# A hybrid two-layer encoder step on one core: the SSM layer's first cluster, its exponents and its state scaling are re-ordered

## The chip, the cores and the metric

The kernel runs on one core of a Trainium2 chip. The metric is the time of one execution on the device, in microseconds (us). A kernel's time is the median of its runs.

A core has a matrix engine (TensorE, PE in the profile), a vector engine (VectorE, DVE), a scalar engine (ScalarE, ACT), a general engine (GpSimd, POOL), and queues that start transfers. Each engine works through its own list of instructions in order. An instruction that waits for another engine holds up everything behind it in its list.

## The reference

The model is one inference step of two layers for 384 tokens: 256 tokens of one prompt and 8 sample streams of 16 tokens. Layer 0 is a gated short convolution beside attention. Layer 1, which the change touches, is a state-space (SSM) mixer in four groups of eight heads. Each layer ends in a convolutional feed-forward. Of layer 1's mixer:

```python
z, xbc, dt_raw = split(h @ w_in)
xbc = silu(causal_dwconv(xbc))              # x: 16 tiles of 128 features, B: 4, C: 4
dt = softplus(dt_raw + dt_bias)
cum = cumsum(dt * a)                        # per head
mix = (C B^T) * exp(cum_q - cum_k) * dt     # causal, inside a chunk
y   = mix @ x + exp(cum) * (C h_in)         # h_in: state that enters the chunk
h   = exp(cum_end) * h + (B * w_end)^T x    # state that leaves it
y   = (y + d_skip * x) * silu(z)
out = rms_norm(y, per group) @ w_out
```

The prompt is worked as two blocks of 128 tokens (b = 0, 1), the eight samples together as a third block (b = 2). Each sample has a state of its own, 128 x 512 values in a group, which is read, scaled, added to and written back.

## The kernel before

All large products are in three parts (high and low halves of activations and weights), so each weight tile of 1,024 columns is split into `wh` (ACT) and `wl` (DVE, line 300) as it arrives. A feature-major product (`xbc`, 24 matmuls of 384 columns) uses one such tile. A `z` projection (72 matmuls of 512 columns) uses four.

Instructions of TensorE in the SSM layer stay in the order of the program text (`T.keep`). Those of the other engines are put in order when the kernel is built, by priority, which is their place in the text unless `tc.high_priority()` raises it.

PSUM has eight banks: three for the large products (`pmm`) and five for all the rest (`paux`), each used in turn. A product therefore waits until the bank's earlier content has been read out ("evicted").

The layer begins with the convolutions of B and C of group 0 (`conv_bc`) and of the first three x tiles (`conv_x`). Then come the exponents: `E` (from `dA` and a masked copy `dAm`), `cT`, whose result goes to memory in `rows` and is read back spread over the partitions as the four `td` tiles (`decays`), and `sgS` from `tjd`. Then `turn_bc(0)`: the products `cb`, evicted into `CB` by DVE, and the transposes `bT`. Then the fourth x tile, B and C of group 1, and `turn_x`, which transposes the four x tiles (`xT`).

Then a loop runs over the groups. In a group, in this order on TensorE:

- the transposes `yT` of the gated output of the group before (`Gate.turn`: read out by ACT into `yh` and by DVE into `yl`);
- `within`: the prompt's state products `S` and the products `y` of each block;
- `inter(2)`: the samples' part `yi`, which reads the eight sample states `h0`;
- `inter(1)`, `turn_bc` and convolutions of the next group, with half of the output product `op` of the group before in group 1;
- `states(0)` and `states(1)`: products `hn`, four banks each. POOL scales a state by its exponent, DVE adds `hn`, and ACT starts the store `o_hs`;
- `project_z` (`z`), then `turn_x`, the scale of the gated output (`factor`), the rest of `op`, and B and C of the group after next.

`skip` loads the next eight states into the same eight buffers and lets POOL make `y` from `xt` and the skip weights. A convolution's `pad` (DVE, from PSUM), its three multiply-adds `c` (DVE, line 303) and its `silu` (ACT, `xf`) follow each `xbc`.

Of the kernel before, what the change touches and what calls it, by code (L numbers as in the profile page):

```python
# [10 lines left out]
F32 = mybir.dt.float32  # L11
# [71 lines left out]
def _pack(x):  # L83
# [47 lines left out]
                blocks.append(wo[kt * P:(kt + 1) * P, c:c + 256])  # L131

    bc(0, 0), bc(1, 0), xs(0), bc(0, 1), bc(1, 1), xs(1), tm(wi, 0)
    bc(0, 2), bc(1, 2), xs(2, (0,)), out(0, (0, 256)), xs(2, (1, 2, 3)), tm(wi, 512), out(0, (512, 768))
    bc(0, 3), bc(1, 3), xs(3), tm(wi, 1024), out(1), tm(wi, 1536), out(2), out(3)
    ffn(1)
    w = np.concatenate(blocks, 1)
# [93 lines left out]
def build(nc, tc, d, stop=None):  # L231
# [119 lines left out]
    class Weights:  # L351
        def __init__(self):
            self.tiles, self.made, self.raw, self.pos = {}, 0, None, 0

            t, self.gain = 32 + 3 * NF + 8, {}
            for g, at in enumerate(((11, 12, 20, 21), range(32, 36), range(40, 44), range(44, 48))):
                self.gain.update({t + i: 4 * g for i in at})
            self.total = d["w"].shape[0] * (RC // WC)

# [620 lines left out]
    def turn_bc(g, Bg, Cg):  # L980

        ps = paux("cb")
        for b in range(3):
            o = slice(b * P, (b + 1) * P)
            T.matmul(ps[:, o], lhsT=Bg[:, o], rhs=Cg[:, o], start=True, stop=True)
        CB = t512("CB", 2, (P, 3, P))
        tt(CB[:, 0:2, :], ps[:, 0:256].rearrange("p (b q) -> p b q", q=P),
           C("T").unsqueeze(1).broadcast_to([P, 2, P]), ALU.mult)
        tt(CB[:, 2, :], ps[:, 256:384], C("Ts"), ALU.mult)
        ps = paux("bT")  # L990
        for b in range(3):
            T.transpose(ps[:, b * P:(b + 1) * P], Bg[:, b * P:(b + 1) * P], ident)
        Bt = t512("Bt", 2, (P, 2, P))
        act(Bt, ps[:, :256].rearrange("p (b n) -> p b n", n=P), AF.Copy)

        Bm = t512("Bm", 2, (P, 2, P))
        for par in range(2):
            act(Bm[:, par, :], ps[:, 256:384], AF.Copy, scale=C("pmask")[:, par:par + 1])
        Cm = Cms[g % 2]
        c4 = Cg[:, 256:384].rearrange("p (j two t) -> p j two t", two=2, t=LB)  # L1000
        for two in range(2):
            G.tensor_copy(Cm[:, two::2, 16 * two:16 * two + 16], c4[:, :, two, :])
        return Cg, Cm, CB, Bt, Bm
# [30 lines left out]
    class Group:  # L1034
# [31 lines left out]
        def skip(self):  # L1066

            self.h0 = []
            for bb in range(NB):
                h0 = t512("h0", 8)  # L1070
                nc.sync.dma_start(out=h0, in_=d["h0"][bb, self.g])
                self.h0.append(h0)
            for b in range(3):
                y = t512("y", 5)
                tt(heads(y[:, :]), heads(self.xt[:, b, :]), bc64(prr("dsk", 32)[:, self.h8]), ALU.mult, G)
                self.ys.append(y)

        def within(self):

            g = self.g  # L1080
            for b in range(3):
                if b < 2:
                    ph = paux("S")
                    T.matmul(ph, lhsT=self.Bt[:, b, :], rhs=self.xw[b], start=True, stop=True)
                    if b == 0:
                        self.S0 = t512("S0", 1)
                        act(self.S0, ph, AF.Copy)
                    else:
                        S1 = self.xt[:, 0, :]
                        tt(heads(S1), heads(self.S0[:, :]), bc64(E[:, 224 + 8 * g:232 + 8 * g]), ALU.mult)  # L1090
                        tt(S1, S1, ph, ALU.add)
                        nc.gpsimd.dma_start(out=d["o_hp"][g], in_=S1)
                py = paux("y")
                for h in range(8):
                    for half in range(2):
                        q = slice(64 * half, 64 * half + 64)
                        T.matmul(py[q, 64 * h:64 * h + 64], lhsT=self.mix[b][h // 4][:, h % 4, q],
                                 rhs=self.xdt[b][:, 64 * h:64 * h + 64], start=True, stop=True)
                tt(self.ys[b], self.ys[b], py, ALU.add)

        def inter(self, b, late=False):

            pi = paux("yi")
            if b == 1:
                T.matmul(pi, lhsT=self.Cg[:, P:2 * P], rhs=self.S0, start=True, stop=True)
            else:

                for par in range(2):
                    for i in range(4):
                        T.matmul(pi[32 * i:32 * i + 32, :], lhsT=self.Cm[:, 2 * i + par, :], rhs=self.h0[2 * i + par],  # L1110
                                 start=par == 0, stop=par == 1)
            yi = self.xt[:, b, :]
            tt(heads(yi), heads(pi[:, :]), bc64(self.col(E, b)), ALU.mult)
            tt(self.ys[b], self.ys[b], yi, ALU.add, None if late else G)

        def states(self, par):

            ph = [paux("hn") for _ in range(4)]
            for i in range(4):
                rows = slice(32 * i, 32 * i + 32)  # L1120
                T.matmul(ph[i], lhsT=self.Bm[rows, par, :], rhs=self.xw[2][rows, :], start=True, stop=True)
            for i in range(4):
                bb = 2 * i + par
                h0, o = self.h0[bb], 256 + 32 * bb + 8 * self.g
                tt(heads(h0[:, :]), heads(h0[:, :]), bc64(E[:, o:o + 8]), ALU.mult, G)
                tt(h0, h0, ph[i], ALU.add)
                nc.scalar.dma_start(out=d["o_hs"][bb, self.g], in_=h0)

# [16 lines left out]
    class Gate:  # L1145
# [13 lines left out]
        def part(self, b, zs):  # L1159
            y = self.ys[b]  # L1160
            tt(y, y, zs[:, b, :], ALU.mult)
            act(t512("yi", 1), y, AF.Square, accum_out=self.ssq[:, b:b + 1])

        def factor(self):
            v = tiny.tile([P, 3], F32, tag="v", name="v")
# [10 lines left out]
        def turn(self, b):  # L1176
            ps = to_features(self.ys[b], "yT")
            o = slice(b * P, (b + 1) * P)
            if self.late:
                for i in range(4):  # L1180
                    yh, yl = self.y2[0][i][:, o], self.y2[1][i][:, o]
                    act(yh, ps[:, i, :], AF.Copy)
                    tt(yl, ps[:, i, :], f32(yh), ALU.subtract)
            else:
                yh, yl = self.y3
                act(yh[:, :, o], ps, AF.Copy)
                tt(yl[:, :, o], ps, f32(yh[:, :, o]), ALU.subtract)

    def add_out(yh, yl, factor):
        for m0 in range(0, 8, 2):  # L1190
            ws = [W.take(256) for _ in range(4)]
            for m in range(2):
# [6 lines left out]
                if factor is None:  # L1199
                    residual(m0 + m, ps)  # L1200
                else:
                    o = t512("y", 5, (P, NT))
                    tt(o, ps[:, :NT], factor, ALU.mult)
                    tt(X[:, m0 + m, :], X[:, m0 + m, :], o, ALU.add)
                    norm_tile(m0 + m, "g_ffn", 1, o1)
# [12 lines left out]
    T.keep = True  # L1218
    Cn = conv_bc(1, 0)
    xs = [conv_x(0, i) for i in range(3)]  # L1220
    dAm = t512("h0", 8, (P, NB, 32))
    tt(dAm, dA[:, 64:96].unsqueeze(1).broadcast_to([P, NB, 32]),
       C("bmask").unsqueeze(2).broadcast_to([P, NB, 32]), ALU.mult)
# [8 lines left out]

    cumK = o0.tile([P, 64], F32, name="cumK")
    V.tensor_copy(cumK, ps[:, 0:64])
    ps = paux("cT")
    for b in range(2):
        T.matmul(ps[0:32, b * P:(b + 1) * P], lhsT=dA[:, 32 * b:32 * b + 32], rhs=C("T"), start=True, stop=True)
    cumQ = o1.tile([32, 256], F32, tag="pad", name="cumQ")
    V.tensor_copy(cumQ, ps[0:32, 0:256])
    rows = dram.tile([2, 32, P], F32, name="rows")  # L1240
    nc.sync.dma_start(out=rows.rearrange("b h q -> h b q"), in_=cumQ.rearrange("h (b q) -> h b q", q=P))
    tt(wdt, E[:, 96:192], dt, ALU.mult)
    tjd = t512("h0", 8, (P, 32, LB))
    tt(tjd, dA[:, 64:96].unsqueeze(2).broadcast_to([P, 32, LB]),
# [3 lines left out]
    act(decS, ps, AF.Exp)  # L1248

    decs = decays(0)  # L1250
    grp = Group(0, decs, turn_bc(0, Bn, Cn))
    xs.append(conv_x(0, 3))
    Bn, Cn = conv_bc(0, 1), conv_bc(1, 1)
    grp.take(turn_x(xs))
    grp.skip()
    xs = [conv_x(1, 0)]
    op = gate = None
    for g in range(4):
        if gate:
            for b in range(3):  # L1260
                gate.turn(b)
            op = add_out(*gate.y2, None)
        last = g == 3
        grp.within()
        grp.inter(2, last)
        if last:
            break
        decs = decays(g + 1)
        if g == 0:
            xs.append(conv_x(1, 1))  # L1270
        elif g == 1:
            steps(op, 16)
        else:
            xs = [conv_x(g + 1, 0)]
        grp.inter(1)
        bc_ = turn_bc(g + 1, Bn, Cn)
        xs.append(conv_x(g + 1, len(xs)))
        grp.states(0)
        while len(xs) < 4:
            xs.append(conv_x(g + 1, len(xs)))  # L1280
        grp.states(1)
        nxt = Group(g + 1, decs, bc_)
        zs = run(project_z())
        gate = Gate(grp.ys, False)
        for b in range(3):
            gate.part(b, zs)
# [5 lines left out]
            steps(op)  # L1292
        if g < 2:
            Bn, Cn = conv_bc(0, g + 2), conv_bc(1, g + 2)
        if g == 0:
            xs = [conv_x(2, 0)]
        grp.skip()

    z = project_z()
# [40 lines left out]
```

## Time and profile before

| what | us |
|---|---|
| runs | 1081.5, 1085.78, 1085.08 |
| median | 1085.08 |
| the profiled execution | 1087.0 |
| its span, first to last instruction | 1085.1 |

The span is the stretch that the profile's rows cover. The profiled execution's own time is 1.9 us longer. Row times count from the span's start. A row's last bracket is the time its engine was idle just before it, and what ended that. "PEclk" is the TensorE clock that was granted, as a share of 2.4 GHz.

### The profile page before, as it was taken

The page shows a single profiled execution, that of the slowest core. Times are in us where ns is not written, and L with a number is a line of the kernel's source. Part 1 is how long each engine was busy: PE and PEld are TensorE (multiplying, and loading weights), DVE is VectorE, ACT ScalarE, POOL GpSimd, SP SyncE. Part 2 cuts the span into 40 slices and gives each one's busy share as a digit, 9 for nine tenths or more (in the row PEclk, how much of TensorE's full clock was granted, in tenths as well). Part 3 has the DMA queues.
Part 4 walks back from the last instruction along what each step waited for, and adds up shares of the span by engine and source line. Part 5 has one row for each costly group of instructions (what it writes and reads, how often), then busy time and mean ns, then how long its engine had stood idle before and what let it go on. Part 6 is the DMA issues. An engine that isn't in the chain of part 4 may idle for free.

```text
span 1085.1 us, 16777 instructions
## 1 busy us (share of the span) xinstructions
PE 1048.3 (97%) x6316; PEld 974.8 (90%) x6316; DVE 739.6 (68%) x1329; ACT 493.6 (45%) x817; POOL 161.7 (15%) x383
## 2 busy tenths in 40 slices
PE   9999999999999999997898999999999999999998
PEld 6788899999999999986776877797899999999998
DVE  7968557776777543486888877975897676765332
ACT  6344334544444433347636556462554444443221
POOL 0030000100000000031824524424001000000000
PEclk9999999999999999998999999999999999999999
DMA  8542443443434444436274363453534434434441
GB/s 281 155 149 72 158 136 117 128 133 120 132 122 132 133 127 128 126 108 187 77 237 150 123 219 127 159 185 106 175 119 123 135 117 125 129 118 143 139 150 42
DMA packets 50328, 150.30 MB, mean 139 GB/s; under 512 B 5992, under 2 KB 8312, under 8 KB 50248
## 3 DMA queue, kind: packets, MB, share of 16 engines
q1 hardware_dynamic: 44360, 136.78, 40.5%
q10 hardware_dynamic: 4608, 8.39, 2.0%
q0 software_dynamic: 1280, 4.06, 1.0%
q8 instruction: 50, 0.82, 0.3%
q14 instruction: 30, 0.25, 0.1%
HBM read 135.81 MB, written 13.40 MB: 138 GB/s over the span
## 4 chain that ended last, share of the span: by engine, by line
PE 37%; DVE 13%; ACT 3%; issue 2%; DMA 2%; SPq 0%; DVEq 0%; POOL 0%; ACTq 0%
PE fg L240 9%; PE fd L240 8%; PE fa L240 8%; PE z L240 5%; DVE wl L300 4%; PE op L240 3%; DVE c L303 2%; ACT wh L306 1%; PE xbc L240 1%; PE yi L240 1%; DVE wl L303 1%; DVE pad L300 1%; PE y L240 1%; DVE X L300 1%; DMA td__4856<-rows 1%
## 5 line engine op out<-in xcount | busy, mean ns | idle before, releaser
L300 DVE TENSOR_TENSOR wl<-raw,wh 128x1024 fp32r<-128x1024 f32 (+1 forms) x205 | 263.5, 1286 | 150.0 <-ACT wh L306 149.5
L306 ACT ACTIVATE wh<-raw 128x1024 fp32r<-128x1024 f32 (+1 forms) x205 | 216.0, 1054 | 225.2 <-PE fd L240 95.0
L240 PE MATMUL fg<-Hh,wh 128*128 128x384 f32 x352 | 119.0, 338 | 1.0 <-DVE pad L300 1.0
L240 PE MATMUL fa<-Hl,wh 128*128 128x384 f32 x352 | 119.3, 339 | 0.5 <-DVE Hl L303 0.5
L240 PE MATMUL fg<-Hl,wh 128*128 128x384 f32 x352 | 119.2, 339 | 0.0
L240 PE MATMUL fa<-Hh,wl 128*128 128x384 f32 x352 | 119.0, 338 | 0.0
L240 PE MATMUL fg<-Hh,wl 128*128 128x384 f32 x352 | 119.0, 338 | 0.0
L240 PE MATMUL fa<-Hh,wh 128*128 128x384 f32 x352 | 118.9, 338 | 0.0
L240 PE MATMUL fd<-hh,wh 128*128 128x384 f32 x352 | 118.3, 336 | 0.0
L240 PE MATMUL fd<-hh,wl 128*128 128x384 f32 x352 | 118.3, 336 | 0.0
L240 PE MATMUL fd<-hl,wh 128*128 128x384 f32 x352 | 118.3, 336 | 0.0
L303 DVE SCALAR_TENSOR_TENSOR c<-pad,prm,c 128x400 f32<-128x400 f32 (+1 forms) x160 | 103.8, 651 | 8.2 <-ACT c L306 6.6
L240 PE MATMUL xbc<-Hh,wh 128*128 128x384 f32 x192 | 67.4, 351 | 0.7 <-DVE X L300 0.7
L240 PEld LDWEIGHTS fg<-Hh,wh 128*128 128x128 f32 x352 | 66.2, 188 | 1.3 <-ACT R L306 1.3
L240 PEld LDWEIGHTS fa<-Hl,wh 128*128 128x128 f32 x352 | 66.1, 188 | 1.1 <-DVE Hl L303 0.9
L240 PE MATMUL xbc<-Hh,wl 128*128 128x384 f32 x192 | 66.3, 345 | 0.0
L240 PEld LDWEIGHTS fa<-Hh,wl 128*128 128x128 f32 x352 | 66.2, 188 | 0.1
L240 PEld LDWEIGHTS fg<-Hl,wh 128*128 128x128 f32 x352 | 66.2, 188 | 0.1
L240 PEld LDWEIGHTS fg<-Hh,wl 128*128 128x128 f32 x352 | 66.2, 188 | 0.1
L240 PEld LDWEIGHTS fa<-Hh,wh 128*128 128x128 f32 x352 | 66.1, 188 | 0.1
L240 PEld LDWEIGHTS fd<-hl,wh 128*128 128x128 f32 x352 | 66.2, 188 | 0.0
L240 PEld LDWEIGHTS fd<-hh,wl 128*128 128x128 f32 x352 | 66.2, 188 | 0.0
(803 smaller groups left out, 2145.8 us busy)
## 6 DMA issues: line engine op xcount, KB each, us to landing
raw<-w SPq DMA_DIRECT2D x219, 512.0 KB, 3.5
kc<-kc SPq DMA_DIRECT2D x8, 256.0 KB, 4.0
vc<-vc SPq DMA_DIRECT2D x8, 256.0 KB, 3.1
X<-x SPq DMA_DIRECT2D x8, 192.0 KB, 4.0
o_y<-X SPq DMA_DIRECT2D x8, 192.0 KB, 2.6
o_v<-vt POOLq DMA_DIRECT2D x3, 256.0 KB, 2.6
o_k<-kraw POOLq DMA_DIRECT2D x3, 256.0 KB, 3.3
cst<-cst SPq DMA_DIRECT2D x1, 617.0 KB, 6.0
```

The lines of the kernel that those rows point to most:

```text
L240: ins = nc.tensor.matmul(*a, **kw)
L300: (eng or V).tensor_tensor(out=out, in0=a, in1=b, op=op)
L303: V.scalar_tensor_tensor(out=out, in0=a, scalar=s, in1=b, op0=op0, op1=op1)
L306: S.activation(out, a, f, **kw)
```

## The change

In words:

- **States.** The scaling of each sample state in `states` moves from POOL to DVE (32 instructions over the four groups).
- **yT last in the first cluster.** `gate.turn` moves behind `within` and `inter(2)` of the next group. For that the `y` tiles get six buffers for five, and `part` writes its squares over `zs`, so that the tile `yi` of its own goes.
- **Exponents a product later.** `turn_bc(0)` and the fourth x tile of group 0 now stand ahead of the exponents, and `cT` with the store to `rows` ahead of `E`.
- **First turned x a product later.** The first x tile of group 1 stands between C of group 1 and `turn_x`, and the second ahead of the loop. Group 0's third and fourth follow at the places of the second and third. In group 0, 12 of the 24 steps of `z` stand between `states(0)` and `states(1)`.
- **Group 1.** Its second x tile comes ahead of `inter(1)`, the 16 steps of `op` after `turn_bc`. The weights are packed in that order.
- **Evictions ahead.** The evictions into `CB`, of `y`, of `yi`, and of `yT` are put in their engines' queues with high priority.

```diff
@@ _pack
-    bc(0, 2), bc(1, 2), xs(2, (0,)), out(0, (0, 256)), xs(2, (1, 2, 3)), tm(wi, 512), out(0, (512, 768))
+    bc(0, 2), bc(1, 2), xs(2, (0, 1)), out(0, (0, 256)), xs(2, (2, 3)), tm(wi, 512), out(0, (512, 768))
@@ turn_bc
-        tt(CB[:, 0:2, :], ps[:, 0:256].rearrange("p (b q) -> p b q", q=P),
-           C("T").unsqueeze(1).broadcast_to([P, 2, P]), ALU.mult)
-        tt(CB[:, 2, :], ps[:, 256:384], C("Ts"), ALU.mult)
+        with tc.high_priority():
+            tt(CB[:, 0:2, :], ps[:, 0:256].rearrange("p (b q) -> p b q", q=P),
+               C("T").unsqueeze(1).broadcast_to([P, 2, P]), ALU.mult)
+            tt(CB[:, 2, :], ps[:, 256:384], C("Ts"), ALU.mult)
@@ skip (and add_out)
-                y = t512("y", 5)
+                y = t512("y", 6)
@@ within
-                tt(self.ys[b], self.ys[b], py, ALU.add)
+                with tc.high_priority():
+                    tt(self.ys[b], self.ys[b], py, ALU.add)
@@ inter
-            tt(heads(yi), heads(pi[:, :]), bc64(self.col(E, b)), ALU.mult)
+            with tc.high_priority():
+                tt(heads(yi), heads(pi[:, :]), bc64(self.col(E, b)), ALU.mult)
@@ states
-                tt(heads(h0[:, :]), heads(h0[:, :]), bc64(E[:, o:o + 8]), ALU.mult, G)
+                tt(heads(h0[:, :]), heads(h0[:, :]), bc64(E[:, o:o + 8]), ALU.mult)
                 tt(h0, h0, ph[i], ALU.add)
                 nc.scalar.dma_start(out=d["o_hs"][bb, self.g], in_=h0)
@@ part
-            act(t512("yi", 1), y, AF.Square, accum_out=self.ssq[:, b:b + 1])
+            act(zs[:, b, :], y, AF.Square, accum_out=self.ssq[:, b:b + 1])
@@ turn
-                act(yh[:, :, o], ps, AF.Copy)
-                tt(yl[:, :, o], ps, f32(yh[:, :, o]), ALU.subtract)
+                with tc.high_priority():
+                    act(yh[:, :, o], ps, AF.Copy)
+                    tt(yl[:, :, o], ps, f32(yh[:, :, o]), ALU.subtract)
@@ ahead of the loop
     xs = [conv_x(0, i) for i in range(3)]
+    bc_ = turn_bc(0, Bn, Cn)
+    xs.append(conv_x(0, 3))
+    ps = paux("cT")
...
+    nc.sync.dma_start(out=rows.rearrange("b h q -> h b q"), in_=cumQ.rearrange("h (b q) -> h b q", q=P))
     dAm = t512("h0", 8, (P, NB, 32))
...
-    ps = paux("cT")
...
-    nc.sync.dma_start(out=rows.rearrange("b h q -> h b q"), in_=cumQ.rearrange("h (b q) -> h b q", q=P))
...
-    grp = Group(0, decs, turn_bc(0, Bn, Cn))
-    xs.append(conv_x(0, 3))
+    grp = Group(0, decs, bc_)
     Bn, Cn = conv_bc(0, 1), conv_bc(1, 1)
+    nx = [conv_x(1, 0)]
     grp.take(turn_x(xs))
     grp.skip()
-    xs = [conv_x(1, 0)]
+    xs = [*nx, conv_x(1, 1)]
@@ the loop
+        last = g == 3
+        grp.within()
+        grp.inter(2, last)
         if gate:
             for b in range(3):
                 gate.turn(b)
             op = add_out(*gate.y2, None)
-        last = g == 3
-        grp.within()
-        grp.inter(2, last)
...
-        if g == 0:
-            xs.append(conv_x(1, 1))
-        elif g == 1:
+        xs.append(conv_x(g + 1, len(xs)))
+        grp.inter(1)
+        bc_ = turn_bc(g + 1, Bn, Cn)
+        if g == 1:
             steps(op, 16)
         else:
-            xs = [conv_x(g + 1, 0)]
-        grp.inter(1)
-        bc_ = turn_bc(g + 1, Bn, Cn)
-        xs.append(conv_x(g + 1, len(xs)))
+            xs.append(conv_x(g + 1, len(xs)))
         grp.states(0)
+        z = project_z()
+        if g == 0:
+            steps(z, 12)
         while len(xs) < 4:
             xs.append(conv_x(g + 1, len(xs)))
         grp.states(1)
         nxt = Group(g + 1, decs, bc_)
-        zs = run(project_z())
+        zs = steps(z)
```

## Rows read from the trace of the kernel before

**Rows 1.** The page: busy time of each engine over the whole span.

```profile
PE 1048.3 (97%) x6316; PEld 974.8 (90%) x6316; DVE 739.6 (68%) x1329; ACT 493.6 (45%) x817; POOL 161.7 (15%) x383
```

**Rows 2.** Busy time by stretch of the SSM layer: length, engines, clock, DMA.

```profile
484.50:520.60 36.10, 27.06 (x141) 24.25 (x140) 25.67 (x46) 25.74 (x51) 10.84 (x25) 0.86 0.52 162
520.60:569.50 48.90, 44.20 (x290) 34.01 (x289) 40.21 (x54) 25.30 (x50) 23.72 (x35) 0.97 0.51 168
...
583.80:643.70 59.90, 52.84 (x347) 42.66 (x348) 47.94 (x78) 34.11 (x70) 22.11 (x37) 0.97 0.55 180
...
661.80:717.00 55.20, 50.76 (x325) 39.94 (x324) 43.80 (x68) 30.47 (x63) 22.63 (x34) 0.94 0.56 187
...
735.20:800.00 64.80, 64.59 (x427) 55.36 (x426) 51.24 (x114) 31.57 (x73) 12.48 (x11) 1.00 0.41 134
484.50:735.20 250.70, 225.09 (x1399) 190.71 (x1398) 199.60 (x328) 144.19 (x289) 97.98 (x146) 0.95 0.50 163
```

**Rows 3.** What TensorE waited for: us in total, times, longest.

```profile
PE z L240 <- DVE pad L300: 5.5, 3, 2.7
PE xT L245 <- ACT xf__4908 L306: 4.4, 1, 4.4
PE hn L240 <- DVE CB__5301 L300: 3.5, 1, 3.5
...
PE S L240 <- DVE yl L300: 2.0, 2, 1.8
PE E L240 <- DVE h__4829 L300: 1.9, 1, 1.9
PE S L240 <- ACT S__5815 L306: 1.8, 1, 1.8
PE sgS L240 <- DVE h__4851 L300: 1.7, 1, 1.7
PE yT L245 <- ACT y__5097 L306: 1.6, 1, 1.6
```

**Rows 4.** TensorE in order of time: first and last of two xbc products (48 matmuls).

```profile
653.47 0.34 PE L240 MATMUL xbc<-Hh,wh 128*128 128x384 f32 x1
...
661.62 0.34 PE L240 MATMUL xbc<-Hh,wl 128*128 128x384 f32 x1
```

**Rows 5.** The vector engine in order of time, at places of all three groups.

```profile
509.56 0.68 DVE L300 TENSOR_TENSOR td__4874<-td__4874,CB__4888 128x512 f32<-128x512 f32 x1
510.16 1.74 DVE L303 SCALAR_TENSOR_TENSOR c<-pad,prm,c 128x408 f32<-128x408 f32 x3
...
535.83 6.30 DVE L300 TENSOR_TENSOR wl<-raw,wh 128x1024 fp32r<-128x1024 f32 x1 [2.01 <-ACT wh L306]
542.05 0.61 DVE L300 TENSOR_TENSOR CB__5301<-cb,cst 128x256 f32<-128x256 f32 x2
...
604.11 4.07 DVE L300 TENSOR_TENSOR wl<-raw,wh 128x1024 fp32r<-128x1024 f32 x1
...
615.27 1.21 DVE L300 TENSOR_TENSOR wl<-raw,wh 128x1024 fp32r<-128x1024 f32 x1
...
616.60 0.67 DVE L300 TENSOR_TENSOR h__5770<-h__5770,hn 128x512 f32<-128x512 f32 x1
617.20 0.67 DVE L300 TENSOR_TENSOR h__5774<-h__5774,hn 128x512 f32<-128x512 f32 x1
...
679.37 5.84 DVE L300 TENSOR_TENSOR wl<-raw,wh 128x1024 fp32r<-128x1024 f32 x1
```

**Rows 6.** POOL in order of time: first and last state scaling of a run, then y.

```profile
535.51 1.04 POOL L300 TENSOR_TENSOR h__5079<-h__5079,E 128x512 f32<-128x512 f32 x1
...
539.79 1.25 POOL L300 TENSOR_TENSOR y__5095<-y__5095,xt__5046 128x512 f32<-128x512 f32 x1
```

**Rows 7.** ACT in order of time: the last xf, and after the store triggers.

```profile
513.62 0.62 ACT L306 ACTIVATE xf__4908<-c 128x256 f32<-128x256 f32 x2 [0.91 <-DVE c L303]
...
620.58 1.28 ACT L306 ACT_TABLE_LOAD   x1 [3.07 <-DVE h__5782 L300]
```

More of the change, by code (lines that the diff above doesn't have):

```diff
@@ L355, in __init__ @@
             t, self.gain = 32 + 3 * NF + 8, {}
-            for g, at in enumerate(((11, 12, 20, 21), range(32, 36), range(40, 44), range(44, 48))):
+            for g, at in enumerate(((12, 13, 20, 21), range(32, 36), range(40, 44), range(44, 48))):
                 self.gain.update({t + i: 4 * g for i in at})
@@ L1201, in add_out @@
                 else:
-                    o = t512("y", 5, (P, NT))
+                    o = t512("y", 6, (P, NT))
                     tt(o, ps[:, :NT], factor, ALU.mult)
@@ L1220, in build @@
     xs = [conv_x(0, i) for i in range(3)]
+    bc_ = turn_bc(0, Bn, Cn)
+    xs.append(conv_x(0, 3))
+    ps = paux("cT")
+    for b in range(2):
+        T.matmul(ps[0:32, b * P:(b + 1) * P], lhsT=dA[:, 32 * b:32 * b + 32], rhs=C("T"), start=True, stop=True)
+    cumQ = o1.tile([32, 256], F32, tag="pad", name="cumQ")
+    V.tensor_copy(cumQ, ps[0:32, 0:256])
+    rows = dram.tile([2, 32, P], F32, name="rows")
+    nc.sync.dma_start(out=rows.rearrange("b h q -> h b q"), in_=cumQ.rearrange("h (b q) -> h b q", q=P))
     dAm = t512("h0", 8, (P, NB, 32))
@@ L1234, in build @@
     V.tensor_copy(cumK, ps[:, 0:64])
-    ps = paux("cT")
[L1236 to L1240, printed above, removed]
-    nc.sync.dma_start(out=rows.rearrange("b h q -> h b q"), in_=cumQ.rearrange("h (b q) -> h b q", q=P))
     tt(wdt, E[:, 96:192], dt, ALU.mult)
@@ L1294, in build @@
             Bn, Cn = conv_bc(0, g + 2), conv_bc(1, g + 2)
-        if g == 0:
-            xs = [conv_x(2, 0)]
+        xs = [conv_x(2, 0)] if g == 0 else []
         grp.skip()
```

## The prediction, made before the changed kernel was run

> **What bounds the kernel now.** I read the page first. TensorE is marked busy for 97% of the span [rows 1], and the feed-forward stages around the SSM layer have no gaps that this change touches. So I asked for busy time by stretch, cut at the places where the SSM layer's TensorE order turns: 484.5 to 520.6 (exponents up to the first `S`), 520.6 to 569.5 (group 0), 583.8 to 643.7 (group 1), 661.8 to 717.0 (group 2), and 735.2 to 800.0 (group 3). The reader is to see two things in [rows 2]. From 484.5 to 735.2 TensorE is busy 225.1 of 250.7 us, so it idles 25.6 us, and its mean clock there is 0.95. And DVE is busy 199.6 of 250.7 us (80%), so the engine that feeds TensorE has little left over. After 735.2 TensorE idles 0.2 us: group 3 has nothing to give.
>
> The idle time by stretch is 36.1 - 27.1 = 9.0, 48.9 - 44.2 = 4.7, 59.9 - 52.8 = 7.1 and 55.2 - 50.8 = 4.4 us, together 25.2 [rows 2].
>
> The table of waits names it [rows 3]. Ahead of group 0 TensorE stands for `dAm` (`h__4829`, 1.9), for `tjd` (`h__4851`, 1.7) and for the last x tile (`xf__4908`, 4.4). In group 0 it stands for the eviction of `CB` (3.5). In groups 1 and 2 it stands for the scaled output before `yT` (1.6), then for banks that `yT` used (`S` behind ACT 1.8, behind `yl` 2.0). In every group `z` stands for the `pad` of the convolution just before it (5.5 in three waits).
>
> Next I asked why those evictions are late, in DVE's order of time. One split of weights, `wl`, takes 1.21 us [rows 5]. At 535.83, 604.11 and 679.37 it takes 6.30, 4.07 and 5.84, which is 12.6 us too much in all. The first of these spans POOL's state scalings (1.04 us each, the first shown at 535.51) and ends with POOL's next work at 539.79 plus 1.25 [rows 6]. `CB` is evicted right behind it, at 542.05 [rows 5]. So here DVE stood while POOL scaled states.
>
> **The change part by part.**
>
> *States on DVE.* Removed from POOL: 32 scalings. Added to DVE: 32. DVE's nearest row is the addition of the same shape, 0.67 long and 0.60 from one start to the next [rows 5]; I take 0.61, so 32 x 0.61 = 19.5 us, 4.9 in a group. Freed on DVE: up to 12.6 us. POOL's additions to `y` stay and can still hold DVE for 1.25 each [rows 6], so I count 12.6 - 3 x 0.6 = 10.8. Net over groups 0 to 2: 14.6 - 10.8 = +3.8 us of DVE work; in group 3 +4.9, hidden, since DVE is busy 51.2 of 64.8 there and TensorE does not wait. The bounds of what a net +3.8 costs TensorE: nothing if it falls in DVE's idle time (20% of the stretch), 3.8 if all of it lands ahead of `z`. I take 1.5.
>
> The row shows one DVE instruction kept out through several POOL instructions in succession. The Trainium skill (SBUF — State Buffer, SBUF: two separate sides) says that the two engines share a port pair as an exclusive lock, held for one whole instruction, with the loser fully blocked. Read strictly, that would cost DVE at most the rest of one 1.04 us scaling at each of the three places, some 3 us in all; the sum by that would be about 2 us less favourable. I go by the row.
>
> *Exponents a product later.* `turn_bc` and one `xbc` product go between the third x tile and the exponents. A product is 4.16 us (its 24 matmuls at 8.15 us over the 47 steps from 653.47 to 661.62) [rows 4]. TensorE's waits for `dAm` and `tjd`, 3.6 us together, fall under this cover, and so does 1.0 us for `dA` that makes up the 9.0. Without the cover they return whole. Nothing new waits on the transfer of `rows`: `cT`, its copy and its store keep their order and come a little sooner.
>
> *First turned x a product later.* `xT` waits 4.4 us for `xf__4908`, which ACT makes at 513.62 [rows 3, 7]. That tile is late because its three multiply-adds start at 510.16, right behind the `td` products on DVE [rows 5]. Now the fourth x tile is made one product earlier (ahead of the exponents) and used one later. Cover is about 7 us for a wait of 4.4. What is late next is DVE: the stretch had 25.7 us of DVE work in 36.1, and it loses about 9 us of waiting and gains the second x tile of group 1. Its length would be 36.1 - 9.0 + 4.2 = 31.3, with 25.7 plus about 2.5 of DVE work, 90%. ACT stands alike at 25.7. I credit 7.5 of the 9.0. Bounds: 4 (only `xT`) to 11.5, the 9.0 with a clock that stays up: it was 0.86 in this stretch [rows 2], and each gap that goes leaves fewer such drops.
>
> *CB ahead in its queue, and z between the states.* The 3.5 us of group 0 had two causes, DVE held by POOL and `CB`'s place behind a `wl`. Both go, and a product now stands ahead of `states(0)`. I credit 3.5, and 0.9 for the same place in group 2 (the rest of its 4.4 is 1.8 for `S` and 1.75 for `z`). Bounds: 2 to 5.5, since a held `wl` can also make weights late.
>
> *yT last.* The scaled outputs get `within` and `inter(2)`, some 7 us of TensorE, as cover: the 1.6 for `yT` and the 1.8 and 2.0 for banks go, 5.4 us. What is late next: five banks turn in order, so the first `yT` needs the first `y`'s bank back, the second that of the second `S`. The `y` additions are now ahead in the queue, that of `S` isn't. I charge 1.0 for it and credit 4.4. Bounds: 2 to 6. Behind a late `yT` stand only convolutions, whose weights are there.
>
> *Group 0's steps of z, the move of `op` in group 1, six y buffers, squares over `zs`.* Same instructions, same counts. The weights are packed in the new order. I cost them at nothing: no row of group 0's or 1's waits names them. Bounds: -0.5 to +1.
>
> *What comes back at z.* `z` waits 5.5 us for `pad`s, which are not raised in priority. TensorE now comes to `z` 3 to 4 us sooner in a group, by the waits above. DVE does not come sooner by as much: it has 40.2 of 48.9 us in group 0 and 4.9 more to do [rows 2]. Bounds: nothing back, or all 8.8 us of groups 0 to 2 (3.5 + 0.9 + 4.4). I take a quarter, 2.2.
>
> **The sum.** -7.5 - 3.5 - 0.9 - 4.4 + 1.5 + 2.2 = -12.6 us from named waits. To this I add the clock: a mean of 0.95 between 1.0 (2.4 GHz) and 0.5 (1.2 GHz) is a tenth of 250.7, 25 us at half pace [rows 2]. That would cost 12.5 if TensorE worked through all of it, but part of it lies in the gaps themselves, and the lowest clock stands where most gaps go. I take 3, bounds 0 to 6. In all -15.6. The profiled execution took 1087.0 us, so it becomes 1071.4. It lay 1.9 above the median, so the median becomes 1069.5. A measurement of this kernel can tell a change of about 0.5%, 5.4 us, from none.
>
> **Rivals.**
>
> *DVE becomes the bound.* 199.6 us of DVE plus 3.8 in a stretch that should shrink by 15.6 to 235 is 87% on the mean, more in the slices around `states`. If three quarters of what is gained in the groups comes back at `z` (6.6 for 2.2) and the prelude gives 4 for 7.5, 1069.5 + 4.4 + 3.5 = 1077.4. For it: the `pad` waits of [rows 3] are DVE's already. Against it: DVE idles 51.1 us in that stretch [rows 2], thirteen times the net addition. The Trainium skill (Perfetto Trace Analysis, Optimizing Scalar/DVE Operations) advises to move work off a saturated DVE, and doubts that a move between DVE and GpSimd helps as they share a port. That speaks for this rival; here the rows decide how near to saturation DVE is. Chance 0.2.
>
> *The evictions gain nothing.* Queue places and POOL's remaining additions leave the groups as they were, and only the prelude gives 7.5 with 1.5 of clock; or the two engines' queues mesh worse. 1085.1 - 7.5 - 1.5 = 1076 at best; with the group's waits moved to other places and half the prelude lost, 1081 (no change that can be told). Chance 0.14 together, 0.12 of it within 0.5%.
>
> *Slower: ACT's store triggers.* ACT idles 3.07 us behind a state's addition, with triggers of stores in its queue and weight splits behind them [rows 7]. A scaling ahead of each addition makes four triggers wait for eight DVE instructions, 4 x 0.61 = 2.4 us more in each of six clusters. It decides once ACT is held for longer than the weights made ahead last, about 4 us of TensorE, which 3.07 + 2.4 exceeds. At full price 6 x 2.4 = 14.6 us on TensorE; DVE, late by the same, takes back the groups' gains, and the prelude's 7.5 stays: 1085.1 + 14.6 - 7.5 = 1092.2. Against it: DVE can do the scalings ahead of `hn`, as POOL did, and then the triggers wait no longer than now. Chance 0.08.
>
> **How the numbers follow.** Forecast 0.58, DVE the bound 0.2, nothing gained in the groups 0.14, slower 0.08. The range's lower end adds the better bounds: prelude 11.5, groups 5.5 and 6, clock 6, nothing for DVE and nothing back at `z`, 29 us, or 1056. Above, it takes in DVE as the bound and half of no change: 1083. Left out are the slower case, some of no change, and a tail below. Faster by over 0.5% is the forecast and DVE as the bound and a little of the third: 0.8; within 0.5% 0.12; slower 0.08.
>
> **What the changed profile would show.** No `wl` above 2.5 us in the groups. No wait of TensorE for `xf` before the first `xT`, none for `CB` over 1 us, none for `yT` in groups 1 and 2. TensorE's idle time before the first `S` down from 9.0 to about 2, and the clock of that stretch above 0.93. DVE's share of the SSM layer near 87%, `z`'s waits for `pad` at 6 to 9 us. The prediction is wrong if `z`'s waits grow beyond 12 us, if `wl` stays long though POOL scales no state, or if ACT idles over 4 us behind state additions.

## The result

The changed kernel takes 1069.24 us in the median (1068.29 to 1072.5, 4 runs) against 1084.52 before (1081.5 to 1085.78, 4 runs). The ratio is 0.9868, 95% interval 0.9838 to 0.9899: faster by 14.3 us, with an interval of about 3.3 us to either side. The forecast was 1069.5. The total fits far better than its terms, as the rest shows.

The profiled execution took 1072.5 us with a span of 1070.5, so 14.6 us less span than before. Not all of that is the change's. The last feed-forward stage, which it does not touch, shows this in two stretches of 50 us, before and after (columns as in [rows 2]):

```profile
850.00:900.00 50.00, 50.00 (x285) 50.00 (x284) 35.09 (x60) 22.80 (x30) 3.75 (x24) 1.00 0.41 125
```

```profile
838.00:888.00 50.00, 50.00 (x290) 50.00 (x289) 35.45 (x60) 22.85 (x31) 3.72 (x24) 1.00 0.42 129
```

TensorE got 285 matmuls through in 50 us before and 290 after, at a full granted clock both times. Over that stage, from its first `fa` (799.65 before, 788.38 after) to the end of the span, this is 285.5 against 282.1 us, 3.4 of the 14.6. In the traces of all twelve kernels of the experiments, b1 among them, which is the kernel before but for one line, the stage takes 281.9 to 282.2 us, so the 3.4 belong to this one profiled execution and not to the change. I leave it out of what follows. Between the first `xbc` of the SSM layer and that `fa` the two traces differ by 12.0 us (340.3 and 328.3).

### The profile page after: what moved, and what is told of

Same layout as the page of the kernel before. It is cut to its first block, busy times and chain, and to the rows that moved or that the text cites. A ratio compares the mean times of both kernels' runs of the same rounds, so it can differ in the third digit from the quotient of the medians.

```text
span 1070.5 us, 16702 instructions
## 1 busy us (share of the span) xinstructions
PE 1039.9 (97%) x6316; PEld 968.5 (90%) x6316; DVE 747.5 (70%) x1361; ACT 503.9 (47%) x825; POOL 133.6 (12%) x351
## 4 chain that ended last, share of the span: by engine, by line
PE 34%; DVE 14%; ACT 4%; issue 2%; DMA 1%; ACTq 0%; POOL 0%; DVEq 0%
PE fd L240 9%; PE fg L240 9%; PE fa L240 8%; PE z L240 4%; DVE c L303 3%; DVE wl L300 2%; PE xbc L240 2%; DVE wl L303 1%; ACT wh L306 1%; DVE X L300 1%; PE y L240 1%; DVE pad L300 1%; DMA raw<-w 1%; PE op L240 1%; ACT L306 1%
## 5 line engine op out<-in xcount | busy, mean ns | idle before, releaser
L300 DVE TENSOR_TENSOR wl<-raw,wh 128x1024 fp32r<-128x1024 f32 (+1 forms) x205 | 252.2, 1231 | 140.4 <-ACT wh L306 139.9
L240 PEld LDWEIGHTS fd<-hh,wh 128*128 128x128 f32 x352 | 66.2, 188 | 0.0
```

Source lines behind the costliest of these rows:

```text
L240: ins = nc.tensor.matmul(*a, **kw)
L300: (eng or V).tensor_tensor(out=out, in0=a, in1=b, op=op)
```

## The profile after

Busy time of the changed kernel, cut at the same places of the work as [rows 2]. The first stretch now also holds the first two x tiles of group 1:

```profile
485.30:518.00 32.70, 30.08 (x164) 27.84 (x163) 22.48 (x42) 27.57 (x52) 8.20 (x22) 0.90 0.64 194
518.00:565.80 47.80, 39.57 (x264) 29.48 (x264) 43.71 (x66) 29.00 (x54) 21.14 (x30) 0.89 0.43 138
579.60:633.50 53.90, 51.26 (x349) 41.46 (x349) 48.37 (x87) 37.58 (x76) 13.28 (x28) 1.00 0.59 193
654.00:705.70 51.70, 48.12 (x326) 38.23 (x325) 44.61 (x76) 32.89 (x65) 15.93 (x25) 0.97 0.62 203
724.20:788.40 64.20, 64.20 (x427) 55.00 (x426) 55.72 (x122) 31.36 (x72) 1.62 (x2) 1.00 0.42 136
485.30:724.20 238.90, 219.77 (x1397) 186.82 (x1397) 203.75 (x352) 154.63 (x297) 81.22 (x123) 0.96 0.53 170
```

TensorE's idle time by stretch was 9.0, 4.7, 7.1 and 4.4 us [rows 2]. It is 32.7 - 30.1 = 2.6, 47.8 - 39.6 = 8.2, 2.6 and 3.6 us now. The stretch ahead of the first `S` lost most of its gaps, groups 1 and 2 lost some of theirs, and group 0 has 3.5 us more than it had, though it has fewer matmuls to do. All in all TensorE idles 238.9 - 219.8 = 19.1 us (25.6 before); the 2.1 that are left lie between the stretches. DVE is at 85% (203.75 of 238.9).

What TensorE waited for in the changed kernel, against [rows 3]:

```profile
PE y L240 <- DVE xdt__5111 L300: 7.9, 1, 7.9
PE z L240 <- DVE pad L300: 3.7, 2, 3.4
PE sgS L240 <- DVE h__4915 L300: 2.4, 1, 2.4
...
PE yi L240 <- ACT S__5785 L306: 1.3, 1, 1.3
...
PE yT L245 <- DVE y__5781 L300: 0.7, 1, 0.7
```

Gone are the waits for `CB`, for the fourth x tile, for `dAm`, and those of `S` behind `yT`. Not gone is the one for `tjd` (`sgS`): it was 1.7 us and is 2.4. New is one long wait: the first `y` of group 0 stands 7.9 us for `xdt`. DVE and POOL around that place, in order of time:

```profile
515.85 0.68 DVE L300 TENSOR_TENSOR td__4938<-td__4938,CB__4833 128x512 f32<-128x512 f32 x1
516.45 6.00 DVE L303 SCALAR_TENSOR_TENSOR c<-pad,prm,c 128x408 f32<-128x408 f32 x5
522.37 2.06 DVE L300 TENSOR_TENSOR wl<-raw,wh 128x1024 fp32r<-128x1024 f32 x1
524.36 1.42 DVE L303 SCALAR_TENSOR_TENSOR c<-pad,prm,c 128x408 f32<-128x408 f32 x1
525.70 0.61 DVE L300 TENSOR_TENSOR pad<-xbc,R 128x256 f32<-128x256 f32 x2
526.23 0.68 DVE L300 TENSOR_TENSOR xdt__5111<-xt__5092,dt 128x512 f32<-128x512 f32 x1
```

```profile
516.83 1.15 POOL L300 TENSOR_TENSOR xw__5113<-xt__5092,wdt 128x512 f32<-128x512 f32 x1 [7.67 <-ACT xt__5092 L306]
517.95 1.38 POOL L300 TENSOR_TENSOR y__5139<-xt__5092,prm 128x512 f32<-128x512 f32 x1
```

ACT has made `xt` by 517.7, but DVE's queue holds six `c`, a `wl` and two `pad` before `xdt`, and POOL's `xw` and `y` run beside them. An undisturbed `c` takes 0.63 long and 0.55 from start to start; here five take 6.00.

The clock fell too. TensorE stood from 519.2 to 527.05, and the granted clock of the 7 us behind the gap was 0.59, between the levels 1.0 (2.4 GHz) and 0.5 (1.2 GHz). Two `S` products took 1.13 us ahead of the gap and 2.08 behind it. In all of group 0 the clock fell from 0.97 to 0.89:

```profile
527.00:534.00 7.00, 6.95 (x102) 5.22 (x106) 6.28 (x12) 3.36 (x11) 2.79 (x7) 0.59 0.40 121
```

```profile
518.04 1.13 PE L240 MATMUL S<-xw__5113,Bt__4840 128*128 128x512 f32 x2 [0.22 <-POOL xw__5113 L300]
528.96 2.08 PE L240 MATMUL S<-xw__5117,Bt__4840 128*128 128x512 f32 x2
```

## The experiments

Every other kernel was timed against the kernel before in one of three series of four kernels. The table gives the ratio to before with its 95% interval, and the difference to the changed kernel at 1.08 us for a thousandth. The changed kernel's own ratio is known to 0.003, so a single difference below some 3 us is not told from none by the table. Within a series the intervals are narrower. The expectations count from 1068 or 1069 us; since the kernel before ran some 2 us shorter in the series (1082.4 to 1082.7), differences are read from the ratios.

| kernel | median us | ratio | interval | to the changed kernel, us |
|---|---|---|---|---|
| changed | 1069.24 | 0.9868 | 0.9838 to 0.9899 | |
| e1_prelude_back | 1072.51 | 0.9904 | 0.9891 to 0.9918 | +3.9 |
| e2_states_pool | 1074.01 | 0.9923 | 0.9910 to 0.9936 | +5.9 |
| e3_no_priority | 1068.24 | 0.9869 | 0.9856 to 0.9881 | +0.1 |
| e4_yT_first | 1071.77 | 0.9901 | 0.9888 to 0.9914 | +3.6 |
| b1_states_dve_only | 1071.48 | 0.9901 | 0.9883 to 0.9919 | +3.6 |
| e5_xdt_ahead | 1066.14 | 0.9854 | 0.9833 to 0.9876 | -1.5 |
| e6_no_scaling | 1064.01 | 0.9830 | 0.9809 to 0.9852 | -4.1 |
| e7_pads_ahead | 1066.89 | 0.9849 | 0.9828 to 0.9870 | -2.1 |
| e8_xdt_and_pads | 1062.56 | 0.9815 | 0.9793 to 0.9838 | -5.7 |
| e9_exponents_back | 1067.52 | 0.9864 | 0.9841 to 0.9887 | -0.4 |
| e10_turn_back | 1070.54 | 0.9889 | 0.9867 to 0.9910 | +2.3 |
| e11_pool_work_on_dve | 1067.81 | 0.9849 | 0.9825 to 0.9873 | -2.1 |

**e2_states_pool.** One part of the change undone:

```diff
-                tt(heads(h0[:, :]), heads(h0[:, :]), bc64(E[:, o:o + 8]), ALU.mult)
+                tt(heads(h0[:, :]), heads(h0[:, :]), bc64(E[:, o:o + 8]), ALU.mult, G)
```

> The changed kernel with the state scalings back on POOL. If DVE stood while POOL scaled states, some wl of 4 to 6 us return, CB is late again and the time rises by 5 to 9 us, to 1074 to 1078. The rival: the order alone does it, DVE gets 19.5 us of work back and z waits less, so the time stays at 1069 or falls to 1065.

It rose by 5.9 us, as the first theory has it. Its trace shows the hold again, in another instruction, a `c`. DVE, and POOL beside it:

```profile
594.64 5.45 DVE L303 SCALAR_TENSOR_TENSOR c<-pad,prm,c 128x408 f32<-128x408 f32 x1
600.02 0.61 DVE L300 TENSOR_TENSOR pad<-xbc,R 128x256 f32<-128x256 f32 x2
```

```profile
594.38 1.28 POOL L300 TENSOR_TENSOR y__5781<-y__5781,xt__5565 128x512 f32<-128x512 f32 x1
595.61 1.04 POOL L300 TENSOR_TENSOR h__5763<-h__5763,E 128x512 f32<-128x512 f32 x1
596.61 1.04 POOL L300 TENSOR_TENSOR h__5767<-h__5767,E 128x512 f32<-128x512 f32 x1
597.62 1.03 POOL L300 TENSOR_TENSOR h__5771<-h__5771,E 128x512 f32<-128x512 f32 x1
598.62 1.04 POOL L300 TENSOR_TENSOR h__5775<-h__5775,E 128x512 f32<-128x512 f32 x1
```

One `c` of 0.63 us lasts from before the second of these POOL instructions until after the last. The rest of the first theory did not come: no `wl` in the groups takes over 2.1 us and TensorE doesn't wait for `CB`. It stands 2.8 us for `X` (in `op`) instead, which DVE comes to some 5 us after the held `c`. So this trace links the 5.9 us to the hold only in part.

**b1_states_dve_only.** The kernel before with this one line changed the other way, and nothing else:

```diff
-                tt(heads(h0[:, :]), heads(h0[:, :]), bc64(E[:, o:o + 8]), ALU.mult, G)
+                tt(heads(h0[:, :]), heads(h0[:, :]), bc64(E[:, o:o + 8]), ALU.mult)
```

> The kernel before with the state scalings moved to DVE and nothing else. If what DVE loses while POOL scales states is worth what its removal gave in the changed kernel, the time falls by 4 to 8 us from 1082.4, to 1074 to 1078, and no wl in the groups takes over 2.5 us. The rival: in the old order the added 19.5 us of DVE work cost as much as they free, 1080 to 1085.

It fell by 10.7 us (0.9901), more than expected, and gives alone three quarters of what the whole change gives. No `wl` in the groups takes over 1.7 us. Its waits of TensorE, in the SSM layer:

```profile
PE xT L245 <- ACT xf__4908 L306: 3.5, 1, 3.5
PE S L240 <- DVE yl L300: 2.0, 2, 1.8
...
PE z L240 <- DVE pad L300: 1.8, 2, 1.1
PE S L240 <- ACT S__5815 L306: 1.8, 1, 1.8
```

The waits of the old order are all there. The one for `CB` is gone, though `CB` (536.41) still stands behind a `wl` (534.66) in DVE's queue, and `z`'s waits fell from 5.5 [rows 3] to 1.8, though DVE was given some 19.5 us more to do. A rival is that POOL's scalings came late in themselves, being slower than DVE's. Against it: the tables of waits show none of TensorE or DVE for POOL in the SSM layer of the kernel before.

**e6_no_scaling.** The scaling left out on either engine, so that the stored states lack their factor:

```diff
-                tt(heads(h0[:, :]), heads(h0[:, :]), bc64(E[:, o:o + 8]), ALU.mult)
```

> The changed kernel with the scaling of the sample states left out altogether, on either engine (the states that are stored lack the factor). Neither POOL's hold on DVE nor DVE's 19.5 us are there. If DVE's added work lands on TensorE's path, the time falls by 4 to 8 us, to 1060 to 1064. If it lies in DVE's idle time, it falls by less than 2, to 1066 to 1068.

It fell by 4.1 us, at the lower edge of the first expectation. So of the 10 us by which POOL's scaling is dearer than none (5.9 + 4.1), DVE's scaling keeps some 4, not far above what the table can tell: the added work isn't free, and POOL's scaling costs more than twice as much.

**e3_no_priority.** The four `with tc.high_priority():` of the change taken out:

```diff
-        with tc.high_priority():
-            tt(CB[:, 0:2, :], ps[:, 0:256].rearrange("p (b q) -> p b q", q=P),
-               C("T").unsqueeze(1).broadcast_to([P, 2, P]), ALU.mult)
-            tt(CB[:, 2, :], ps[:, 256:384], C("Ts"), ALU.mult)
+        tt(CB[:, 0:2, :], ps[:, 0:256].rearrange("p (b q) -> p b q", q=P),
+           C("T").unsqueeze(1).broadcast_to([P, 2, P]), ALU.mult)
+        tt(CB[:, 2, :], ps[:, 256:384], C("Ts"), ALU.mult)
...
```

> The changed kernel with none of the four evictions raised in priority. If their place in the queue matters, TensorE waits again for CB or for banks of yT, and the time rises by 3 to 6 us, to 1072 to 1075. The rival: the queue's order was never the cause, only what held DVE, and the time stays within 1.5 us of 1069.

Nothing changed (0.9869 for 0.9868), as the rival has it. Its trace has no wait for `CB` and waits of 2.1 us at `yT` in all (1.0 in the changed kernel). On `CB`'s place it tells little: in group 0 `CB` (538.44) stands ahead of the next `wl` (539.00) without the priority too. e1, e2 and e4 ran in the same series, and each lies 0.0032 to 0.0054 above it, outside the intervals.

**e4_yT_first.** `yT` ahead again:

```diff
-        grp.within()
-        grp.inter(2, last)
         if gate:
             for b in range(3):
                 gate.turn(b)
             op = add_out(*gate.y2, None)
+        grp.within()
+        grp.inter(2, last)
```

> The changed kernel with yT ahead of within and inter(2) again. By the prediction (credit 4.4) the waits of yT, S and y return in groups 1 and 2 and the time rises to 1073 to 1075. The rival: z, which waits for DVE, then waits less by as much, and the time stays at 1069 to 1071.

It rose by 3.6 us, close to the lower end of the first expectation (3.8). The old waits are back:

```profile
PE S L240 <- DVE yl L300: 3.9, 2, 2.0
...
PE yT L245 <- ACT y__5141 L306: 1.6, 1, 1.6
```

**e1_prelude_back, e9_exponents_back, e10_turn_back.** The stretch ahead of the loop in its old order, whole and by halves. e9:

```diff
     xs = [conv_x(0, i) for i in range(3)]
-    bc_ = turn_bc(0, Bn, Cn)
-    xs.append(conv_x(0, 3))
-    ps = paux("cT")
...
     act(E, ps, AF.Exp)
...
+    ps = paux("cT")
...
-    grp = Group(0, decs, bc_)
+    grp = Group(0, decs, turn_bc(0, Bn, Cn))
+    xs.append(conv_x(0, 3))
```

e10:

```diff
-    nx = [conv_x(1, 0)]
     grp.take(turn_x(xs))
     grp.skip()
-    xs = [*nx, conv_x(1, 1)]
+    xs = [conv_x(1, 0), conv_x(1, 1)]
```

e1 is both.

> The changed kernel with the stretch ahead of the loop in the order of before: exponents straight behind the third x tile, turn_bc and the fourth x tile behind them, the first turned x ahead of the first x tile of group 1. All else as changed. By the prediction, which credits 7.5 us to this part, the time rises from 1069 to about 1076.5. By the trace of the changed kernel, where the first y waits 7.9 us for xdt and the loop's second product starts no earlier than before, the part gives nothing or costs up to 3: 1066 to 1070.

> The changed kernel with the exponents straight behind the third x tile again, the first turned x still a product later. Both halves undone gave +3.9. If the cover for dAm, tjd and dA (4.6 us of waits) is what counts, 1071 to 1073. If the cover for the first xT (4.4) is what counts, 1068 to 1069.

> The changed kernel with the first turned x ahead of the first x tile of group 1 again, the exponents still a product later. By the first theory of the run before, 1068 to 1069, since the fourth x tile is early anyway and xdt on DVE is then asked for sooner; by the second, 1071 to 1073.

e1 rose by 3.9, between the two expectations: the part is worth about half of the 7.5 credited. Its waits:

```profile
PE z L240 <- DVE pad L300: 6.3, 2, 3.4
PE xT L245 <- ACT xf__4908 L306: 3.6, 1, 3.6
PE E L240 <- DVE h__4829 L300: 1.8, 1, 1.8
PE sgS L240 <- DVE h__4851 L300: 1.7, 1, 1.7
```

The waits of the old order are back, and the 7.9 us of `y` for `xdt` are gone. One of `z`'s two waits, 2.87 us, is in group 0, where the changed kernel has 0.3. e9 and e10 point to the first turned x as the half that counts (+2.3 against -0.4), but both differences lie inside the interval, so this is not shown. Their waits of `y` for `xdt` are 4.0 and 6.9 us. In e9 the waits for `dAm`, `tjd` and `dA` return, 1.9, 1.7 and 0.8, and `y` waits 3.9 us less than in the changed kernel: most of what the later exponents save ahead of `S`, TensorE gives back at `y`.

**e5_xdt_ahead, e7_pads_ahead, e8_xdt_and_pads.** The changed kernel with more raised in priority. e5 has the first of these hunks, e7 the second, e8 both:

```diff
-                tt(heads(xdt[:, :]), x3, bc64(self.col(dt, b)), ALU.mult)
+                with tc.high_priority():
+                    tt(heads(xdt[:, :]), x3, bc64(self.col(dt, b)), ALU.mult)
...
-        tt(pp_[:, 3:], ps[:, 0:256], R[:, 0:256], ALU.mult)
-        tt(ps_[:, :, 3:], tok_s(ps[:, 256:384]), tok_s(R[:, 256:384]), ALU.mult)
+        with (tc.high_priority() if 4 <= i < 16 else ExitStack()):
+            tt(pp_[:, 3:], ps[:, 0:256], R[:, 0:256], ALU.mult)
+            tt(ps_[:, :, 3:], tok_s(ps[:, 256:384]), tok_s(R[:, 256:384]), ALU.mult)
```

> The changed kernel with the xdt multiplications raised in priority, so that the 7.9 us wait of the first y should go. If that wait is a matter of DVE's order, the time falls by 4 to 7 us, to 1061 to 1064. If DVE as a whole is behind in group 0, what is put off for xdt is missed later: the wait of y goes below 2 us, the waits of z or hn in group 0 grow by as much, and the time stays within 2 us of 1068.

> The changed kernel with the pad evictions of the x tiles of groups 1 to 3 raised in priority. z waits for just these. If queue order sets z's waits, its 3.7 us go and the time falls by 2 to 4 us, to 1064 to 1066. If DVE is behind as a whole, or z's losses come from its weights, the time stays within 1.5 us of 1068.

> The changed kernel with both the xdt multiplications and the pad evictions of the x tiles of groups 1 to 3 raised in priority. Each alone gave about 2 us or less. If the two waits are separate (the first y and the third part of z), the gains add: 1064 to 1065. If both draw on the same backlog of DVE, one takes back what the other gives: 1066 to 1068.

e5 took 1.5 us off and e7 2.1, both within the interval. e5's trace says in part why so little came of 7.9 us:

```profile
PE z L240 <- DVE pad L300: 3.4, 1, 3.4
PE yi L240 <- ACT S__5785 L306: 2.2, 1, 2.2
...
PE hn L240 <- DVE xt__5092 L300: 1.5, 1, 1.5
```

The wait for `xdt` is gone, but `hn` now waits in group 0 for what DVE put off, and in group 1 `yi` waits 2.2 us for ACT's copy of `S`, where it waited 1.3. Together, e8, the two gave 5.7 us, to 1062.56: more than either theory's sum, and the best version here, at 0.9815 (0.9793 to 0.9838), whose interval meets that of the changed kernel only at its edge. Its `z` waits are down to 1.0 us, and one wait of 6.8 is left, in group 1, for ACT's copy of `S`. ACT had itself stood 5.5 us for DVE (`rqo`) shortly before. In the stretch with the same work as 485.3 to 724.2 of the changed kernel, DVE is at 204.59 of 228.90 us, 89%:

```profile
PE yi L240 <- ACT S__5785 L306: 6.8, 1, 6.8
...
PE z L240 <- DVE pad L300: 1.0, 2, 0.6
```

```profile
485.20:714.10 228.90, 216.26 (x1397) 183.47 (x1396) 204.59 (x351) 151.70 (x295) 79.81 (x123) 0.98 0.54 178
```

**e11_pool_work_on_dve.** Two more of POOL's multiplications on DVE:

```diff
-                tt(heads(xw[:, :]), x3, bc64(self.col(wdt, b)), ALU.mult, G)
+                tt(heads(xw[:, :]), x3, bc64(self.col(wdt, b)), ALU.mult)
...
-                tt(heads(y[:, :]), heads(self.xt[:, b, :]), bc64(prr("dsk", 32)[:, self.h8]), ALU.mult, G)
+                tt(heads(y[:, :]), heads(self.xt[:, b, :]), bc64(prr("dsk", 32)[:, self.h8]), ALU.mult)
```

> The changed kernel with the multiplications of xw and of the skip part of y on DVE too (24 more instructions, 24 x 0.61 = 14.6 us of DVE work in four groups, and up to 17 us fewer that DVE is held by POOL). If POOL's hold on DVE costs more than the work itself here as well, the time falls by 1 to 4 us, to 1064 to 1067. If these are overlapped well now and DVE is near its limit, it rises by 2 to 6 us, to 1070 to 1074.

The median is 1067.81, the ratio 2.1 us better, inside the interval: a gain isn't shown, and of the loss in the second expectation nothing is seen. Its DVE tells the rest, in the stretch from 486.5 to 719.85, which begins and ends at the same work as 485.3 to 724.2 of the changed kernel:

```profile
486.50:719.85 233.35, 217.87 (x1398) 185.48 (x1397) 200.28 (x375) 151.38 (x295) 51.32 (x100) 0.97 0.54 175
```

DVE ran 23 instructions more than in the changed kernel's 238.9 us and was busy 3.5 us less (200.28 for 203.75). The place ahead of the first `y` shows where this comes from:

```profile
516.14 2.85 DVE L303 SCALAR_TENSOR_TENSOR c<-pad,prm,c 128x408 f32<-128x408 f32 x5
518.92 1.22 DVE L300 TENSOR_TENSOR wl<-raw,wh 128x1024 fp32r<-128x1024 f32 x1
520.05 0.64 DVE L303 SCALAR_TENSOR_TENSOR c<-pad,prm,c 128x408 f32<-128x408 f32 x1
521.14 0.68 DVE L300 TENSOR_TENSOR xdt__5111<-xt__5092,dt 128x512 f32<-128x512 f32 x1
```

With POOL out of the way the six `c`, the `wl` and the two `pad` take 5.0 us from the first `c` to `xdt`, against 9.8 in the changed kernel. So some 4.8 us of the wait of `y` there is POOL's hold again, now by `xw` and the skip part of `y`. The wait for `xdt` is gone, and TensorE stands 5.0 us for `xw` at the first `S` instead.

## Why the prediction was right, and where its terms were not

**States on DVE: right mechanism, mis-sized.** The forecast charged 1.5 us for the move and credited 4.4 under the eviction of `CB`. Alone it gave 10.7 us (b1); undone in the changed kernel it cost 5.9 (e2). The step that failed is the one that set 10.8 us freed on DVE against 14.6 added in groups 0 to 2 and let the rest land on TensorE. The 12.6 us were lost at three places, each in one held instruction. In groups 0 and 2 the eviction of `CB`, for which TensorE stood (3.5 and 0.9), came right behind it; in group 1 no wait stands directly behind it, and the link to `z`'s wait of 2.7 there is argued. The 14.6 are spread over the groups, and some 4 us of all the added work reach TensorE (e6). An average over DVE's busy time weighs the two alike. They are not. That b1 and the rest of the change (e2: 8.3 us by its ratio) sum to 19 and not 14.3 suggests that they remove partly the same waits; on top of the states the rest gives 3.6, about what the table can tell.

The Trainium skill (SBUF — State Buffer, SBUF: two separate sides) describes the hold as a lock kept for one whole instruction. e2's 5.45 us through several POOL instructions agrees that the loser is blocked and not slowed, and shows more than one instruction's worth. So do the three long `wl` of the kernel before: they end at 542.13, 608.18 and 685.21 [rows 5], each 1.1 us (about one `wl`) behind the end of POOL's run, at 541.04 [rows 6], 607.08 and 684.12. The forecast read the first as ending with POOL's work; it ran after it.

```profile
606.03 1.05 POOL L300 TENSOR_TENSOR h__5784<-h__5784,E 128x512 f32<-128x512 f32 x1
682.84 1.28 POOL L300 TENSOR_TENSOR y__6558<-y__6558,xt__6315 128x512 f32<-128x512 f32 x1
```

Where the Trainium skill weighs an offload between the two engines (Perfetto Trace Analysis, Optimizing Scalar/DVE Operations), its doubt that moving work to GpSimd helps is borne out: here work moved the other way, onto an engine at 80%, gained 10.7 us.

**CB ahead in its queue: the step failed.** The forecast named two causes, POOL's hold and the place behind a `wl`. b1 removes the wait for `CB` with `CB` still behind a `wl`, so the first cause alone was enough. e3 adds that the four priorities gain nothing, but as `CB` is ahead of the `wl` there too, it doesn't test the place. The credit of 4.4 belonged to the states.

**Exponents and first turned x: the mechanism held, half the size.** Idle time ahead of the first `S` fell from 9.0 to 2.6, and `xT` no longer waits. `tjd`, which the forecast put under the cover, still does: 2.4 of the 2.6. The forecast said "what is late next is DVE", charged 1.5 for it, and looked for it ahead of `S`, with DVE at 90%. There DVE was at 69% (22.48 of 32.70). The loss came right behind, where `y` now waits 7.9 us for `xdt`. The step that failed is that charge: it counted DVE's load and left out that POOL's `xw` and skip part of `y` hold DVE just there, some 4.8 us by e11. e1 gives 3.9 for the whole part, known to some 3. The clock that was to stay above 0.93 was 0.90.

**yT last: right.** Credited 4.4, measured 3.6 (e4), with the waits where they were expected.

**What comes back at z: not borne out as stated.** 2.2 were charged on top of 5.5. `z` waits 3.7 us in all for `pad`, less than before and less than the 6 to 9 foreseen. The states alone bring it to 1.8 (b1), and with the rest of the change it is 3.7: some 1.9 come back, but from a lower start. That DVE's backlog sets what is left is shown by e6 (1.4 without the scalings) and e7 (0.6 with the `pad`s raised).

**The clock.** 3 us were counted. The mean rose only from 0.95 to 0.96, for what the first stretch gained (0.86 to 0.90) group 0 lost behind its new gap (0.97 to 0.89). No run here takes the clock apart from the gaps, so the 3 us are not shown.

**The signs.** No `wl` over 2.06 us in the groups, no wait for `xf` or `CB`: as said. At `yT` in group 1, 1.0 us is left. The wait for `xdt` was not foreseen. The store triggers did not decide: in groups 0 to 2 ACT idles at most 3.7 us behind a state addition, under the sign's 4. One wait of 5.7 in group 3 is over it, and TensorE doesn't idle there (64.20 of 64.20). With single parts undone, 3.9 + 5.9 + 3.6 + 0.1 = 13.5 of 14.3 us are found, each known to some 3, against the forecast's 15.6 in other shares: too much for the prelude and `CB`, too little for the states. That the total came out within 0.3 us of the forecast is luck: its errors cancelled.

## What to carry to other kernels

When one engine's instruction is several times its usual length, look at what its neighbour runs at that time before counting loads: an instruction held where the chain passes can cost more than as much work spread out, and adding work to the busier engine can be the cheaper choice. When a stall is removed ahead of an engine near its limit, find the next thing that is due from it and price that too. In these runs a raised priority paid only for results that TensorE stood for: the four of the change gained nothing that can be told (e3), while `xdt` and the `pad`s, two results it did wait for, gave 5.7 us together (e8).

## What the runs showed that I had not expected

Two patterns of DVE beside POOL stand in the traces. Beside `xw` and `y` the two took turns: five `c` in 6.00 us, with POOL's instructions stretched to 1.38. Beside state scalings that followed each other every 1.00 us, DVE got no turn until the run ended: 6.30 in [rows 5], 5.45 in e2. But in e2, from 533.48 to 535.46, two `c` got through between scalings of 1.34 and 1.38, so the kind of work alone doesn't decide. What does was not tried. The hold works the other way too: in the changed kernel an addition of POOL's, 1.30 at its next, took 4.59 us beside DVE's run of scalings and ended 1.1 us after it.

```profile
536.65 4.59 POOL L300 TENSOR_TENSOR y__5143<-y__5143,xt__5092 128x512 f32<-128x512 f32 x1 [3.43 <-DVE xt__5092 L300]
541.73 1.30 POOL L300 TENSOR_TENSOR y__5141<-y__5141,xt__5092 128x512 f32<-128x512 f32 x1 [0.17 <-DVE xt__5092 L300]
```

```profile
539.44 0.69 DVE L300 TENSOR_TENSOR h__5129<-h__5129,E 128x512 f32<-128x512 f32 x1
```

The pace of the last feed-forward stage, 285 or 290 matmuls in 50 us at a full granted clock, differed between the profiled execution of the kernel before and all the others; its cause is open.
